# The dilated mixer's tokens ordered by class of 4, and the keys and values of two dilations packed in one block

## The chip, the cores and the metric

The kernel runs on one core of a Trainium2 chip. The metric is the device time of one execution in microseconds (us), the median of three runs. Engines: PE (TensorE matmul; its weight loads are listed apart as PEld), DVE (VectorE), ACT (ScalarE), POOL (GpSimd) and SP (SyncE, which issues most transfers).

## What is computed

A trunk of two layers over 256 tokens of width 2048, 16 heads of 128. Layer 0 is a dilated sliding-window mixer, layer 1 a block-sparse one that with 256 tokens is plain causal attention. Around each: RMS norm, a modulation computed from the vector c, a gate, and at the end a final RMS norm. All inputs are fp32.

```python
DSWA_PATTERNS = ((128, 1), (512, 4), (2048, 16))       # (window, dilation), one per head group

def dilated_mixer(h, w_in, slopes):
    parts = jnp.split(h @ w_in, 3 * N_GROUPS + 1, axis=-1)   # q, k, v of three groups, and z
    for g, (window, dilation) in enumerate(DSWA_PATTERNS):
        o, lse = dilated_window_attention(q_g, k_g, v_g, window, dilation, slopes)
    alpha = jax.nn.softmax(jnp.stack(lses), axis=0)
    o = jnp.einsum('gbsh,gbshd->bshd', alpha, jnp.stack(outs))
    return o * jax.nn.silu(parts[-1])
...
for i in range(DEPTH):
    h = rms_norm(x, norm_w[i]) * (1.0 + scale) + shift
    y = (dilated_mixer(h, a_w_in) if i == 0 else moba_mixer(h, b_w_in)) @ w_out
    x = x + gate * y
return rms_norm(x, final_norm_w)
```

Query t of a group with dilation d attends to t, t-d, t-2d, and so on. Mixing the three groups by their denominators is the same as one softmax over the keys of all three, and the kernel does that.

## The kernel before

**Products.** Nearly all work on PE is the projection of the tokens with fp32 weights. Each operand is split into a high part and a rest (`wh` and `wl`, `hA[.., 0]` and `hA[.., 1]`), and three products in fp32r make one exact enough product. A weight unit of 512 KB is loaded by SP into `raw`, ACT makes `wh` (line 342) and DVE makes `wl` (line 348). The program is a list of steps, each a handful of products on PE; other work (`tasks`, `first_tasks`) is attached to steps by number with `at` and `at_once`, so the order on every engine is that of the code as it is run through at the end (lines 818 to 826).

**Parts and groups of heads.** The 16 heads come in four groups j of four. For every group ten parts are made: v0, v1, v2, z, q0, k0, q1, k1, q2, k2 (the list `PARTS`). A v part has tokens on the partitions (tokens are the stationary operand, `moving`, lines 268 to 270), all others have the head's 128 elements there (`stationary`, 279 to 281, and `stationary_heads`, 292 and 297). The order in `PARTS` sets both the order of work and the buffer that a part lies in. The products sum up in four PSUM banks, `acc`, two for a part at a time (four, one a head, in `stationary_heads`).

**The first 330 us.** The rows of hA appear one after another, since DVE has to sum up the modulation first (`mod_unit`, line 142; `rows_ready`, lines 245 to 257). Until then, parts of the groups 0 and 1 (v0 to k0 of group 1) are worked on in visits: as many rows as are ready for one part, then the next part. At a visit's end `evac_visit` copies the two banks into the part's buffer with ACT (line 560, first visit) or adds them with DVE (line 562, later visits). The first eight visits are one step long each. Later parts are evacuated by `evac` (line 567, ACT).

**An item of the dilated layer.** `item_a` handles one head and one half of the tokens: tt = 0 has the 128 even tokens, tt = 1 the odd ones, so that x is loaded as `x[0].rearrange("(m a) d -> m a d", a=2)`. There are 32 items. A key at a distance that is a multiple of 4 or 16 lies in the same half, so an item has four blocks of 128 keys: both halves for group 0, its own half for group 1 and its own half for group 2. In step s0 PE makes the scores (line 438, into `pss`), DVE adds the distance mask `dm` scaled by the head's slope (401), takes the maximum (403), and ACT the exponent (406). In s1 DVE normalises (414). In s2 PE transposes the four blocks (419) and ACT copies them (421). In s3 PE multiplies them with the values (456, into `po`), DVE gates (458), and `split` writes the two parts of y (189 on ACT, 190 on DVE). The four steps stand apart by the offsets of `item_a`. The items of group 0 stand in the first stretch of group 1, and so on; those of group 3 stand in the output projection.

Of the 128x128 scores of group 1 in such a block only those at a distance of a multiple of 4 count, that is half; for group 2 (multiple of 16) an eighth. The rest is masked.

Of the kernel before, what the change touches and what calls it, by code (L numbers as in the profile page):

```python
# [18 lines left out]
P = 128  # L19
# [13 lines left out]
def distance_masks():  # L33
# [3 lines left out]

    m = np.arange(P)

    def block(tq, tk, rule):  # L40
# [5 lines left out]
    even, odd, low, high = 2 * m, 2 * m + 1, m, m + P  # L46
    cols = [block(even, even, near), block(even, odd, near), block(even, even, every(4)), block(even, even, every(16)),
            block(odd, even, near), block(odd, odd, near)]
# [5 lines left out]
def trunk_kernel(ctx: ExitStack, tc: tile.TileContext, x, c, small_w, mod_t, weights, final_norm_w, dmask, out, laid_out):  # L54
# [23 lines left out]
    x_v = x[0].rearrange("(m a) d -> m a d", a=2)  # L78
# [13 lines left out]
    dm = const.tile([P, 9 * P], F32, name="dm")  # L92
# [93 lines left out]
    def split(dst, src):  # L186

        hi = dst[:, :, 0]
        nc.scalar.activation(hi, src, AF.Copy)
        nc.vector.tensor_tensor(dst[:, :, 1], src, hi.bitcast(F32), op=ALU.subtract)  # L190
# [233 lines left out]
    def item_a(j, hh, tt, base, offsets):  # L424
# [4 lines left out]
        blocks = [(0, slice(0, S)), (1, tok), (2, tok)]  # L429
        order = blocks if tt == 0 else blocks[1:] + blocks[:1]  # L430
        parts = [slice(0, 512)]

        def s0():
            ps = ps_s.tile([P, 512], F32, name="pss", tag="s")
            n = 0
            for g, ks in order:
                w = ks.stop - ks.start
                nc.tensor.matmul(ps[:, n:n + w], heads_of("A", j, f"q{g}")[:, hh, tok],  # L438
                                 heads_of("A", j, f"k{g}")[:, hh, ks], start=True, stop=True)
                n += w  # L440
            st["t"] = tp.tile([P, 512], F32, name="t")
            st["l"] = bias_exp(ps, dm[:, 256 * tt:256 * tt + 512], SLOPES[head], parts, st["t"])
# [4 lines left out]
        def s2():  # L447
            st["pT"] = transpose_p(st["t"], 4)

        def s3():  # L450
            po = ps_o.tile([P, 512], F32, name="po", tag="o")
            vs = []
            for g, ks in order:
                vs += [tokens_of("A", j, f"v{g}", hh)[:, a] for a in ((0, 1) if g == 0 else (tt,))]
# [4 lines left out]
            split(y_of("A", j)[:, hh:hh + 1, :, tt::2], y[:, None, 0:P])  # L459
# [4 lines left out]
    def item_b(j, hh, base, offsets):  # L464
# [5 lines left out]
        def s0():  # L470
# [5 lines left out]
            st["l"] = bias_exp(ps, dm[:, 768:1152], SLOPES[head], parts, st["t"])  # L476
# [22 lines left out]
    PARTS = ["v0", "v1", "v2", "z", "q0", "k0", "q1", "k1", "q2", "k2"]  # L499
# [55 lines left out]

# [309 lines left out]
```

## Time and profile before

| | |
|---|---|
| median of 3 runs | 1576.88 us (1575.72 to 1578.0) |
| the profiled execution | 1577.62 us |
| its span in the trace | 1575.6 us |
| PE busy | 1553.2 us (99%) |
| DVE busy | 1123.7 us (71%) |
| ACT busy | 759.9 us (48%) |
| moved by DMA | 380.77 MB, mean 242 GB/s |

Busy times are unions of the instructions' intervals. A matmul's record is longer than the time after which the next one can start, since matmuls are pipelined; the cost of a matmul is read from the distance between starts. An fp32 matmul (not fp32r) leaves two records on PE and two on PEld, a transpose one on each. In a timeline, equal instructions that follow one another are merged into one row with their number.

### The profile page before, as it was taken

To read this page: it belongs to the slowest core of one execution; us is meant where nothing else is said; L and a number is where in the kernel's file an instruction comes from. 1 tells how busy PE (TensorE), PEld (TensorE's weight loads), DVE (VectorE), ACT (ScalarE), POOL (GpSimd) and SP (SyncE) were. 2 spreads that over 40 slices of the span, in tenths; PEclk is the share of its full clock that TensorE was granted. 3 is DMA by queue.
4 is the path that set the end of the run, shared out by engine and by line. 5 is a ranking of instruction groups with operands and counts; after the bars stand their busy time and mean duration, and the time that the engine had idled before them with its cause. 6 is when DMAs were issued, how large, how long until landed. Compare 5 with 4: busy or idle time off the path is not lost.

```text
span 1575.6 us, 23685 instructions
## 1 busy us (share of the span) xinstructions
PE 1553.2 (99%) x8958; PEld 1363.6 (87%) x8958; DVE 1123.7 (71%) x1998; ACT 759.9 (48%) x1049; POOL 32.2 (2%) x35
## 2 busy tenths in 40 slices
PE   8999999999999999999999999999999999999997
PEld 6898899998988888888888888887888888888886
DVE  7889888978767766677766675766458788565665
ACT  7644444444435544444544444554445555455543
POOL 5000000000000000000000000000000000000000
PEclk9999999999999999999999999999999999999998
DMA  9988998875888567877577876465367897855553
GB/s 349 344 284 311 319 316 277 287 262 191 267 228 323 182 213 250 286 258 259 191 233 259 278 264 209 137 222 168 134 201 233 290 319 253 229 176 199 186 174 107
DMA packets 104758, 380.77 MB, mean 242 GB/s; under 512 B 11714, under 2 KB 11842, under 8 KB 104388
## 3 DMA queue, kind: packets, MB, share of 16 engines
q1 hardware_dynamic: 102528, 372.95, 70.9%
q0 software_dynamic: 1536, 5.26, 0.9%
q8 instruction: 70, 1.15, 0.3%
q10 hardware_dynamic: 580, 1.06, 0.2%
q14 instruction: 44, 0.36, 0.1%
HBM read 377.10 MB, written 2.11 MB: 241 GB/s over the span
## 4 chain that ended last, share of the span: by engine, by line
PE 87%; DVE 3%; ACT 1%; DMA 1%; issue 1%; POOL 0%; POOLq 0%; DVEq 0%; ACTq 0%
PE acc L292 27%; PE acc L297 14%; PE acc L270 10%; PE acc L268 10%; PE acc L269 10%; PE acc L280 4%; PE acc L281 4%; PE acc L279 4%; PE po L456 1%; PE pss L438 1%; PE pst L419 1%; DVE wl L348 1%; DMA raw<-in_weights_dram 1%; PE po L489 1%; PE pss L473 1%
## 5 line engine op out<-in xcount | busy, mean ns | idle before, releaser
L342 ACT ACTIVATE wh<-raw 128x1024 fp32r<-128x1024 f32 (+1 forms) x505 | 527.4, 1056 | 521.8 <-PE acc L292 180.2
L348 DVE TENSOR_TENSOR wl<-raw,wh 128x1024 fp32r<-128x1024 f32 (+1 forms) x505 | 609.7, 1221 | 204.7 <-ACT wh L342 203.6
L292 PE MATMUL acc<-hA,wh 128*128 128x512 f32 x1152 | 288.3, 392 | 1.4 <-DVE actA1q L543 1.4
L292 PEld LDWEIGHTS acc<-hA,wh 128*128 128x128 f32 x1152 | 207.0, 189 | 38.2 <-DVE actA1q L543 1.7
L292 PE MATMUL acc<-hB,wh 128*128 128x512 f32 x768 | 196.4, 395 | 0.0
L279 PE MATMUL acc<-hA,wh 128*128 128x256 f32 x640 | 182.8, 286 | 1.0 <-ACT hA L251 1.0
L280 PE MATMUL acc<-hA,wh 128*128 128x256 f32 x640 | 182.0, 284 | 0.7 <-DVE hA L257 0.6
L281 PE MATMUL acc<-hA,wl 128*128 128x256 f32 x640 | 181.8, 284 | 0.0
L297 PEld LDWEIGHTS acc<-hA,wl 128*128 128x128 f32 x1152 | 157.3, 190 | 11.7
L297 PE MATMUL acc<-hA,wl 128*128 128x256 f32 x1152 | 160.7, 282 | 0.0
L292 PEld LDWEIGHTS acc<-hB,wh 128*128 128x128 f32 x768 | 137.5, 189 | 24.0
L268 PE MATMUL acc<-wh,hA 128*128 128x512 f32 x384 | 155.5, 405 | 1.6 <-DVE hA L253 1.6
L270 PE MATMUL acc<-wh,hA 128*128 128x512 f32 x384 | 151.0, 393 | 0.3 <-DVE hA L257 0.2
L269 PE MATMUL acc<-wl,hA 128*128 128x512 f32 x384 | 150.9, 393 | 0.0
L142 DVE CUSTOM_DVE_ANT_0 raw<-raw,cb 128x512 f32<-128x512 f32 x198 | 131.2, 689 | 9.9 <-DMA raw<-in_mod_t_dram 9.9
L279 PEld LDWEIGHTS acc<-hA,wh 128*128 128x128 f32 x640 | 123.5, 193 | 1.4 <-ACT hA L251 1.2
L280 PEld LDWEIGHTS acc<-hA,wh 128*128 128x128 f32 x640 | 123.4, 193 | 1.3 <-DVE hA L257 1.0
L281 PEld LDWEIGHTS acc<-hA,wl 128*128 128x128 f32 x640 | 123.5, 193 | 0.0
L297 PEld LDWEIGHTS acc<-hB,wl 128*128 128x128 f32 x768 | 105.2, 190 | 8.4 <-DVE wl L348 0.3
L297 PE MATMUL acc<-hB,wl 128*128 128x256 f32 x768 | 108.3, 283 | 0.1
L270 PEld LDWEIGHTS acc<-wh,hA 128*128 128x128 f32 x384 | 72.5, 189 | 16.7 <-DVE hA L257 1.2
L268 PEld LDWEIGHTS acc<-wh,hA 128*128 128x128 f32 x384 | 72.6, 189 | 16.3 <-ACT hf L254 2.4
(228 smaller groups left out, 1779.6 us busy)
## 6 DMA issues: line engine op xcount, KB each, us to landing
raw<-in_weights_dram SPq DMA_DIRECT2D x512, 512.0 KB, 4.5
raw<-in_mod_t_dram SPq DMA_DIRECT2D x132, 512.0 KB, 4.7
gate<-in_mod_t_dram SPq DMA_DIRECT2D x40, 512.0 KB, 5.4
dm<-in_mod_t_dram SPq DMA_DIRECT2D x20, 512.0 KB, 5.1
xin<-in_x_dram SPq DMA_DIRECT2D x2, 1024.0 KB, 6.0
gate<-gate_rows POOLq DMA_DIRECT2D x4, 512.0 KB, 8.4
x<-in_x_dram POOLq DMA_DIRECT2D x4, 512.0 KB, 7.5
fw<-in_final_norm_w_dram POOLq DMA_DIRECT2D x2, 512.0 KB, 5.4
```

The lines of the kernel that those rows point to most:

```text
L142: nc.vector.tensor_tensor_reduce(part, part, cb[q], 1.0, 0.0 if q else mbT[:, m:m + 1], ALU.mult, ALU.add, modq[:, m, q:q + 1])
L268: nc.tensor.matmul(o, hi, wh[:, i], start=f, stop=False, skip_group_check=True)
L269: nc.tensor.matmul(o, hi, wl[:, i], start=False, stop=False, skip_group_check=True)
L270: nc.tensor.matmul(o, lo, wh[:, i], start=False, stop=l, skip_group_check=True)
L279: nc.tensor.matmul(o, wh[:, i, wc], hi, start=first and h % 2 == 0, stop=False, skip_group_check=True)
L280: nc.tensor.matmul(o, wh[:, i, wc], lo, start=False, stop=False, skip_group_check=True)
L281: nc.tensor.matmul(o, wl[:, i, wc], hi, start=False, stop=last, skip_group_check=True)
L292: nc.tensor.matmul(ps_of(h), ws[u][0][:, i, cols(h)], both, start=us[u] == 0 and i == 0, stop=low_first and us[u] == 7 and i == 1, skip_gr ...
L297: nc.tensor.matmul(ps_of(h)[:, 0:S], ws[u][1][:, i, cols(h)], st(2 * us[u] + i)[:, 0, :], start=False, stop=not low_first and us[u] == 7 a ...
L342: nc.scalar.activation(wh[:, c], raw[:, c], AF.Copy)
L348: nc.vector.tensor_tensor(wl[:, c], raw[:, c], wh[:, c].bitcast(F32), op=ALU.subtract)
L419: nc.tensor.transpose(pt[:, b * P:(b + 1) * P], t[:, b * P:(b + 1) * P], ident)
```

## The change

The 256 tokens of the two halves are put in another order: within a half (even or odd tokens), first the 64 tokens with t mod 4 = a, then the 64 with t mod 4 = 2 + a. Two tokens at a distance that is a multiple of 4 or 16 are now always in the same 64. For the groups 1 and 2 therefore only scores of 64 queries with 64 keys are made, and the four 64x64 results of an item are packed into one block of 128x128: for the first 64 queries (class 0) the keys of group 1 and then those of group 2, for the second 64 (class 1) those of group 2 and then those of group 1. An item has three blocks rather than four.

The values of the groups 1 and 2 are packed to match. The buffer of v1 gets the 64 rows of class 0 of both groups, the buffer of v2 those of class 1. `pieces` yields for each PSUM bank of v1 or v2 the two halves of 64 partitions with their destinations, and both `evac_visit` and `evac` go through them, so such a bank is evacuated by two instructions rather than one. In `PARTS`, z moves up to stand behind v0, so v1 and v2 follow each other with z ahead of them. x is loaded by four transfers of 64 partitions instead of two of 128, and y is written back with a stride of four tokens and not two.

```diff
-    even, odd, low, high = 2 * m, 2 * m + 1, m, m + P
+    by_class = [4 * (m % 64) + 2 * (m // 64) + a for a in range(2)]
+    even, odd, low, high = *by_class, m, m + P
...
-    x_v = x[0].rearrange("(m a) d -> m a d", a=2)
+    x_v = x[0].rearrange("(s b a) d -> a b s d", a=2, b=2)
...
-        blocks = [(0, slice(0, S)), (1, tok), (2, tok)]
-        order = blocks if tt == 0 else blocks[1:] + blocks[:1]
-        parts = [slice(0, 512)]
+        parts = [slice(0, 384)]
+        own, pack = (0, 2) if tt == 0 else (1, 0)
+
+        def classes():
+
+            for b in range(2):
+                for g in (1, 2):
+                    n = 64 * ((g - 1) ^ b)
+                    yield b, g, slice(tt * P + 64 * b, tt * P + 64 * b + 64), slice(pack * P + n, pack * P + n + 64)
 
         def s0():
             ps = ps_s.tile([P, 512], F32, name="pss", tag="s")
-            n = 0
-            for g, ks in order:
-                w = ks.stop - ks.start
-                nc.tensor.matmul(ps[:, n:n + w], heads_of("A", j, f"q{g}")[:, hh, tok],
-                                 heads_of("A", j, f"k{g}")[:, hh, ks], start=True, stop=True)
-                n += w
+            nc.tensor.matmul(ps[:, own * P:own * P + S], heads_of("A", j, "q0")[:, hh, tok],
+                             heads_of("A", j, "k0")[:, hh, 0:S], start=True, stop=True)
+            for b, g, ks, to in classes():
+                nc.tensor.matmul(ps[64 * b:64 * b + 64, to], heads_of("A", j, f"q{g}")[:, hh, ks],
+                                 heads_of("A", j, f"k{g}")[:, hh, ks], start=True, stop=True, skip_group_check=True)
...
-            st["pT"] = transpose_p(st["t"], 4)
+            st["pT"] = transpose_p(st["t"], 3)
...
-            for n, vv in enumerate(vs):
-                nc.tensor.matmul(po[:, 0:P], vv, st["pT"][:, n], start=n == 0, stop=n == 3)
+            v = tokens_of("A", j, "v0", hh)
+            for b in range(2):
+                c = slice(64 * b, 64 * b + 64)
+                nc.tensor.matmul(po[:, c], tokens_of("A", j, f"v{1 + b}", hh)[:, tt], st["pT"][:, pack, c], start=b == 0,
+                                 stop=False, skip_group_check=True)
+            for a in range(2):
+                nc.tensor.matmul(po[:, 0:P], v[:, a], st["pT"][:, own + a], start=False, stop=a == 1,
+                                 skip_group_check=True)
...
-    PARTS = ["v0", "v1", "v2", "z", "q0", "k0", "q1", "k1", "q2", "k2"]
+    PARTS = ["v0", "z", "v1", "v2", "q0", "k0", "q1", "k1", "q2", "k2"]
...
+    def pieces(l, j, p, ps, n):
+
+
+        if l == "A" and p in ("v1", "v2"):
+            for b, t in enumerate((act_of(l, j, "v1"), act_of(l, j, "v2"))):
+                r = 64 * (b if p == "v1" else 1 - b)
+                yield t[r:r + 64, n * GC:(n + 1) * GC], ps[64 * b:64 * b + 64]
+        else:
+            yield act_of(l, j, p)[:, n * GC:(n + 1) * GC], ps
```

The order of instructions on PE at the first item's scores (q and k of group 0 of heads; the number behind a name is the buffer's), before:

```order
L270 MATMUL acc<-wh,hA 128x512
L438 MATMUL pss<-actA0k_356,actA0q_332 128x256
L438 MATMUL pss<-actA0k_411,actA0q_387 128x128
L438 MATMUL pss<-actA0k_505,actA0q_461 128x128
L268 MATMUL acc<-wh,hA 128x512
```

and now:

```order
L278 MATMUL acc<-wh,hA 128x512
L449 MATMUL pss<-actA0k_362,actA0q_338 128x256
L452 MATMUL pss<-actA0k_417,actA0q_393 64x64
L452 MATMUL pss<-actA0k_511,actA0q_467 64x64
L452 MATMUL pss<-actA0k_417,actA0q_393 64x64
L452 MATMUL pss<-actA0k_511,actA0q_467 64x64
L276 MATMUL acc<-wh,hA 128x512
```

Two matmuls of 128x128 have become four of 64x64, of which the second pair writes the PSUM partitions from 64 on. On PE at the first item's outputs, with the next item's transposes behind them, before:

```order
L270 MATMUL acc<-wh,hA 128x512
L456 MATMUL po<-pT,actA0v_246 128x128 x2
L456 MATMUL po<-pT,actA0v_260 128x128
L456 MATMUL po<-pT,actA0v_279 128x128
L419 MATMUL pst<-ident,t 128x128 x4
L268 MATMUL acc<-wh,hA 128x512
```

and now:

```order
L289 MATMUL acc<-hA,wl 128x256
L468 MATMUL po<-pT,actA0v_287 128x64
L468 MATMUL po<-pT,actA0v_288 128x64
L471 MATMUL po<-pT,actA0v_248 128x128 x2
L427 MATMUL pst<-ident,t 128x128 x3
L287 MATMUL acc<-hA,wh 128x256
```

The packed values come first and move 64 columns each, and one transpose is gone. On ACT at the first visits (the evacuations of v0, v1, v2 and z of group 0, among the conversions `wh` and the copies of the transposed x), before:

```order
L560 ACTIVATE actA0v_246<-acc 128x512 x2
L560 ACTIVATE actA0v_260<-acc 128x512 x2
L342 ACTIVATE wh<-raw 128x1024
L560 ACTIVATE actA0v_279<-acc 128x512 x2
L238 ACTIVATE xnT_104<-pxt 128x3x128 x2
L560 ACTIVATE actA0z<-acc 128x512 x2
L342 ACTIVATE wh<-raw 128x1024
L560 ACTIVATE actA0q_332<-acc 128x512 x2
```

and now:

```order
L587 ACTIVATE actA0v_248<-acc 128x512 x2
L587 ACTIVATE actA0z<-acc 128x512 x2
L350 ACTIVATE wh<-raw 128x1024
L587 ACTIVATE actA0v_287<-acc 64x512
L587 ACTIVATE actA0v_288<-acc 64x512
L587 ACTIVATE actA0v_287<-acc 64x512
L587 ACTIVATE actA0v_288<-acc 64x512
L246 ACTIVATE xnT_104<-pxt 128x3x128 x2
L587 ACTIVATE actA0v_287<-acc 64x512
L587 ACTIVATE actA0v_288<-acc 64x512
L587 ACTIVATE actA0v_287<-acc 64x512
L587 ACTIVATE actA0v_288<-acc 64x512
```

z now comes ahead of v1 and v2, and each of these two has four evacuations instead of two.

## Rows read from the trace of the kernel before

**Rows 1.** The page: engines' busy time, and the shares of the last chain.

```profile
PE 1553.2 (99%) x8958; PEld 1363.6 (87%) x8958; DVE 1123.7 (71%) x1998; ACT 759.9 (48%) x1049; POOL 32.2 (2%) x35
...
PE 87%; DVE 3%; ACT 1%; DMA 1%; issue 1%; POOL 0%; POOLq 0%; DVEq 0%; ACTq 0%
```

**Rows 2.** Windows: length, then each engine's busy us (instructions), granted clock, DMA, GB/s.

```profile
20.00:30.00 10.00, 10.00 (x69) 9.24 (x68) 10.00 (x17) 9.81 (x19) 10.00 (x5) 0.93 0.94 342
...
80.00:90.00 10.00, 10.00 (x86) 10.00 (x85) 10.00 (x19) 4.57 (x5) 0.00 (x0) 1.00 0.70 248
90.00:100.00 10.00, 8.43 (x55) 8.03 (x55) 8.77 (x22) 3.10 (x4) 0.00 (x0) 0.83 0.97 337
...
300.00:310.00 10.00, 10.00 (x86) 10.00 (x85) 9.85 (x15) 4.55 (x5) 0.00 (x0) 1.00 0.80 266
...
380.00:390.00 10.00, 8.37 (x68) 7.81 (x66) 7.65 (x18) 4.27 (x7) 0.00 (x0) 1.00 0.52 172
...
560.00:740.00 180.00, 180.00 (x1018) 157.74 (x1018) 119.85 (x202) 80.34 (x100) 0.00 (x0) 1.00 0.76 256
```

**Rows 3.** Timeline of PE at an item's scores, then outputs and transposes: start, length.

```profile
335.28 1.04 PE L438 MATMUL pss<-actA0k,actA0q 128*128 128x256 f32 x6
...
336.39 0.39 PE L269 MATMUL acc<-wl,hA 128*128 128x512 f32 x1
...
349.14 0.39 PE L270 MATMUL acc<-wh,hA 128*128 128x512 f32 x1
349.37 1.05 PE L456 MATMUL po<-pT,actA0v 128*128 128x128 f32 x8
350.26 0.60 PE L419 MATMUL pst<-ident,t 128*128 128x128 f32 x4
...
350.93 0.40 PE L269 MATMUL acc<-wl,hA 128*128 128x512 f32 x1
```

**Rows 4.** Timeline where PE restarts, and durations by line (ns, minimum/median/maximum).

```profile
388.34 0.38 PE L456 MATMUL po<-pT,actA0v 128*128 128x128 f32 x1 [0.54 <-ACT pT L421]
388.34 0.19 PEld L456 LDWEIGHTS po<-pT,actA0v 128*128 128x128 f32 x1 [0.75 <-ACT pT L421]
388.45 0.19 PEld L456 LDWEIGHTS po<-pT,actA0v 128*128 128x128 f32 x1
390.16 0.30 PE L419 MATMUL pst<-ident,t 128*128 128x128 f32 x1 [0.66 <-DVE t L414]
390.13 0.20 PEld L419 LDWEIGHTS pst<-ident,t 128*128 128x128 f32 x2 [0.82 <-PE po L456]
...
L456 PE MATMUL po<-pT,actA0v x64: 270/275/377, 349.4 to 395.7; 128*128 128x128 f32 x64
L419 PEld LDWEIGHTS pst<-ident,t x176: 138/141/144, 343.7 to 1501.8; 128*128 128x128 f32 x176
```

**Rows 5.** Groups of instructions by line and shape: busy us, mean ns of one.

```profile
L403 DVE TENSOR_REDUCE m<-t 128x1 f32<-128x512 f32 x32 | 22.0, 686 | 1.1
L401 DVE SCALAR_TENSOR_TENSOR t<-dm,pss 128x512 f32<-128x512 f32 x32 | 21.9, 685 | 18.4 <-PE pss L438 18.3
L562 DVE TENSOR_TENSOR actA0v<-actA0v,acc 128x512 f32<-128x512 f32 x18 | 11.6, 683 | 1.1 <-PE acc L270 1.1
L401 DVE SCALAR_TENSOR_TENSOR t<-dm,pss 128x384 f32<-128x384 f32 x16 | 8.8, 553 | 8.2 <-PE pss L473 8.2
L560 ACT ACTIVATE actA0v<-acc 128x512 f32<-128x512 f32 x6 | 3.3, 593 | 0.2
```

**Rows 6.** Timeline of DVE and ACT at 94 us.

```profile
94.27 0.16 DVE L148 TENSOR_REDUCE modc<-modq 128x2 f32<-128x8 f32 x1
...
94.66 0.60 ACT L251 ACTIVATE hA<-xnT,modc,sc 128x256 fp32r<-128x256 f32 x1 [2.25 <-DVE sc L247]
```

**Rows 7.** Timeline of SP and DVE at the start.

```profile
1.17 0.92 SPq L796 DMA_DIRECT2D xin<-in_x_dram  x2
...
10.21 0.75 DVE L142 CUSTOM_DVE_ANT_0 raw<-raw,cb,smalls 128x512 f32<-128x512 f32 x1 [1.02 <-ACT cb L111]
```

More of the change, by code (lines that the diff above doesn't have):

```diff
@@ L45, in distance_masks @@
     every = lambda n: (lambda d: (d >= 0) & (d % n == 0))
-    even, odd, low, high = 2 * m, 2 * m + 1, m, m + P
-    cols = [block(even, even, near), block(even, odd, near), block(even, even, every(4)), block(even, even, every(16)),
-            block(odd, even, near), block(odd, odd, near)]
+    by_class = [4 * (m % 64) + 2 * (m // 64) + a for a in range(2)]
+    even, odd, low, high = *by_class, m, m + P
+    packed = np.empty((P, P), np.float32)
+    for b in range(2):
+        r = slice(64 * b, 64 * b + 64)
+        t = even[r]
+        for n, rule in enumerate((every(4), every(16))[::1 - 2 * b]):
+            packed[r, 64 * n:64 * n + 64] = block(t, t, rule)
+    cols = [block(even, even, near), block(even, odd, near), packed, block(odd, even, near), block(odd, odd, near)]
     cols += [block(q, k, lambda d: d >= 0) for q, k in ((low, low), (high, low), (high, high))]
@@ L91, in trunk_kernel @@
     gate = [const.tile([P, 1024], F32, name=f"gate{i}") for i in range(2)]
-    dm = const.tile([P, 9 * P], F32, name="dm")
+    dm = const.tile([P, 8 * P], F32, name="dm")
     ones = const.tile([P, P], F32, name="ones")
@@ L184, in rstd_of, with split @@
         return r
-    def split(dst, src):
-        hi = dst[:, :, 0]
+    def split(dst, src, low=None):
+        parts = [dst[:, :, i] if low is None else dst[:, i] for i in range(2)]
+        hi = parts[0]
         nc.scalar.activation(hi, src, AF.Copy)
-        nc.vector.tensor_tensor(dst[:, :, 1], src, hi.bitcast(F32), op=ALU.subtract)
+        nc.vector.tensor_tensor(parts[1], src, hi.bitcast(F32), op=ALU.subtract)
     start_r = []
@@ L475, in s0 @@
             st["t"] = tp.tile([P, 512], F32, name="t")
[L476 removed]
+            st["l"] = bias_exp(ps, dm[:, 640:1024], SLOPES[head], parts, st["t"])
         def s1():
@@ L554, in whole_part @@
         return i
[L556 to L562 removed]
+    def pieces(l, j, p, ps, n):
[5 more added lines that the diff above has]
+            yield act_of(l, j, p)[:, n * GC:(n + 1) * GC], ps
+    def evac_visit(key, j, p, first):
+        for n, bank in enumerate(groups[key]):
+            for dst, ps in pieces("A", j, p, bank, n):
+                if first:
+                    nc.scalar.activation(dst, ps, AF.Copy)
+                else:
+                    nc.vector.tensor_tensor(dst, dst, ps, op=ALU.add)
     def evac(l, j, p):
[L565 to L567 removed]
+        for n, bank in enumerate(groups[l, j, p]):
+            for dst, ps in pieces(l, j, p, bank, n):
+                nc.scalar.activation(dst, ps, AF.Silu if p[0] == "z" else AF.Copy)
     def silu_in_place(l, j, p):
@@ L795, in trunk_kernel @@
     for tt in range(2):
-        nc.sync.dma_start(xin[tt], x_v[:, tt])
+        for b in range(2):
+            nc.sync.dma_start(xin[tt][64 * b:64 * b + 64], x_v[tt, b])
     start_rstd(0)
```

18 lines of the change are left out of this document (4 added, 14 removed).

## The prediction

> **What bounds the kernel now.** I read the busy shares of the engines first, then the table by stretches, then single items of the dilated layer on TensorE. PE is busy 99% of the span, and 87% of the chain that ended last is PE; DVE has 3% of it [rows 1]. By stretches, PE is busy in the whole of 560 to 740 us, with DVE at two thirds and ACT below half [rows 2]: there, a nanosecond of PE is a nanosecond of the end, and nothing that DVE or ACT saves is worth anything. The granted clock is 1.00 (2.4 GHz) in all stretches but the first and the one at 90 us. Two kinds of place are different. From 20 to 30 us ACT is nearly full, and at 80 to 90 us DVE is completely full; PE then stands for part of 90 to 100 us. And at 380 to 390 us PE is idle for 1.6 us, because the first eight items hang on DVE there: at 390 us PE waits for the normalised scores of line 414 [rows 4]. So the change has to be costed as PE time in the items, and as ACT and DVE time in the first 400 us.
>
> **What an item costs PE.** The dilated layer has 32 items. One fp32 matmul is two records on PE. In rows 3 the scores start at 335.28 us and the second product behind them at 336.39 us; with 0.23 us for the product between (349.14 to 349.37), the three score matmuls cost 0.88 us. The four output matmuls are 8 records from 349.37 to 350.26 us: 0.111 us each. The four transposes are one record each, 0.11 us apart. I need to know whether 0.111 us is the time of the moving columns or of loading the weights. Rows 4 tell it, at 388.34 us, where PE had stood idle: the first weight load begins at 388.34, its matmul lasts 0.38 us instead of the usual 275 ns, so it waited some 0.10 us for the weights, and the second load begins 0.11 us after the first. A 128-column weight load therefore takes 0.107 us by itself, as much as 128 moving columns. For a transpose it is less: after the idle time at 390.13 us two loads of 141 ns span 0.20 us, so they stand 0.06 us apart.
>
> **Step 1, one transpose less.** Each item transposes three blocks of 128 instead of four: 32 x 0.109 = -3.5 us of PE. This is the only sure gain.
>
> **Step 2, the outputs.** The two packed output matmuls move 64 columns instead of 128, but their weights (the values) are still 128 columns wide. Their four records go from 0.107 us of streaming to 0.053 us, while loading the next weights still takes 0.107 us. With the load as the floor [rows 4], 8 records remain at 0.11 us: 0. If the load did not hold, it would be -4 x 0.053 x 32 = -6.8 us; I take 0, since the idle start shows the load alone.
>
> **Step 3, the packed scores.** Two matmuls of 128x128 (4 records, 4 x 0.111 = 0.445 us) become four of 64x64 (8 records). Moving 64 columns takes half of 0.107 us; no row shows a 64-column load, so a record lies between 0.054 us (half of everything) and 0.109 us (a load as long as that of 128 columns). The nearest row is the short load of the transposes, 0.06 us apart [rows 4]; with it, 8 x 0.060 = 0.48 us. Per item that is +0.035 us, between -0.01 and +0.43.
>
> **Step 4, two changes of the array's shape.** The 64x64 matmuls write 64 PSUM partitions each, at 0 or at 64, so they use half of the array's columns; every item goes into that shape and out of it again. The trace shows no such change among busy records: the kernel before has only full-width ones once its products run. The lower bound is the change between fp32 records and the products, which costs nothing: from 349.37 to 350.93 us stand 8 output records, 4 transposes and one product, 1.56 us, and 12 x 0.111 + 0.23 is 1.56 [rows 3]. The upper bound is that PE runs empty and starts again at each change: a record lasts 275 ns while the next would start after 0.111 us, so the tail is 0.165 us, and behind it the first weights load openly, 0.107 us for 128 columns and 0.054 us for 64 [rows 4]. That is 2 x 0.165 + 0.107 + 0.054 = 0.49 us an item. I take the middle, 0.25 us: the load cannot be pulled ahead across the change, and a part of the tail is not waited for. The Trainium skill, "TensorEngine Tiling (Array Packing)", Key Properties, says that a change of tiling mode (not merely of the tile) makes TensorE drain; no row of this trace shows one. By it step 4 would cost the upper bound, by rows 3 nothing.
>
> Steps 1 to 4 make -0.109 + 0 + 0.035 + 0.25 = +0.176 us an item on PE.
>
> **Step 5, where the items stand.** 24 items lie in stretches where PE is full: 24 x 0.176 = +4.2 us. The first eight lie between 335 and 397 us, where DVE carries the chain and PE has 1.6 us of idle time [rows 2]; 8 x 0.176 = 1.4 us of PE fits in there. On DVE each item gets shorter: 384 columns instead of 512 save 0.13 us in the scaled bias (685 against 553 ns) and, by an estimate in the same proportion, as much in the maximum (686 ns) [rows 5], together 8 x 0.26 = -2.1 us, and something in the normalisation. But in the same stretch the two value parts of the second group of heads are now added in four pieces each instead of two, +4 x 0.68 = +2.7 us of DVE. So this stretch I put at 0, between -1.6 and +2 us.
>
> **Step 6, the values' evacuations.** No row shows a piece of 64 partitions; it takes between half of one of 128 and the whole. Durations in rows 5 follow the elements per partition, so I take the whole: 0.6 us on ACT and 0.68 us on DVE. The change has 16 more of them on ACT and 20 more on DVE. Eight of those on ACT belong to the third and fourth group of heads; there the next part's products hide them (the nearest bank is wanted again two heads, some 2.8 us, later); were they not hidden, they would cost up to 8 x 0.6 = 4.8 us. The first four are the trouble: the first visits of the two parts are one step each (six products, 6 x 0.23 = 1.4 us), and their evacuations take 2.4 us instead of 1.2 us on an ACT that is 98% busy from 20 to 30 us [rows 2]. PE must wait for the two banks, or for the hidden rows and weights that ACT makes later: up to +2.4 us. On DVE the next additions of these two parts grow by 4 x 0.68 = 2.7 us; they stand shortly ahead of the stretch in which DVE has no gap, at the end of which PE waits for hA (DVE has summed up the modulation's last pieces by 94.27 us, ACT starts hA at 94.66) [rows 6]. The two delays don't add: a late PE meets late rows there. I take +2 us for both. Later, at 300 to 310 us (DVE 98% [rows 2]), four more additions fall into short visits; +1.5 us, between 0 and 4. Together +3.5 us, between 0 and +7.
>
> **Rest.** Loading x in four transfers rather than two adds two issues of 0.46 us each on SP ahead of the first modulation rows; DVE's first sum of them, at 10.21 us, waits for cb [rows 7], so I put it at 0, at most +0.9 us. The gated output written with a stride of four tokens, the shorter exponent and the shorter copy of the transposed block lie on ACT and DVE beside a full PE: 0.
>
> **Sum.** +4.2 + 0 + 3.5 = +7.7 us. The profiled execution took 1577.62 us (span 1575.6), the median of the runs is 1576.88, less than 0.1% apart, so I add to the median: 1584.6 us.
>
> **Rivals.** (a) The shape changes cost nothing. An item then costs PE -0.074 us, 24 of them -1.8 us, and with step 6 the time is 1578.6 us, inside 0.2%. For it: the fp32 to product change is free in rows 3. (b) PE runs empty at each change, 0.49 us: -0.109 + 0.035 + 0.49 = +0.416 an item, 24 of them +10.0, the first eight no longer fit into PE's idle time (8 x 0.416 - 1.6 = +1.7), with step 6 +15.2: 1592.1 us. For it: a load for half the array cannot sit beside the weights of the full one. The Trainium skill's sentence on the drain, named in step 4, is this rival. (c) Faster: the two column halves run beside each other, so that the packed scores cost 4 x 0.054 instead of 0.445 us (-0.23), with no emptying; with the transpose -0.34 us an item, 24 x -0.34 = -8.1, the first stretch -1.6, step 6 at +3.5: 1570.7 us. It decides once a half's load starts under the other half's matmul. Against it: the records of PE follow one another in every row read. The Trainium skill, same page, Key Properties, says that different tiles can load and multiply in parallel; no run here shows it yet. (d) A 64-column load takes as long as one of 128: step 3 +0.43 us; with free changes 24 x 0.32 = +7.7, with step 6 1588 us.
>
> **Chances.** Forecast (half-priced changes) 0.32, (a) 0.24, (b) 0.20, (c) 0.16, (d) 0.08. A difference under 0.2% (3.2 us) cannot be told from none. A part of (a) falls below it with a small step 6, so: faster 0.20, same 0.25, slower 0.55. The range reaches from (c) to (b): 1570 to 1593 us.
>
> **What would show it.** The number of records from the first 64x64 matmul to the next product, and the gap ahead of each of the two changes (step 4: 0.05 to 0.2 us each if right, 0.2 to 0.27 in (b), none in (a)); the spacing of the eight 64-column records (step 3: 0.06 us); output records still 0.11 us apart though they move 64 columns (step 2; 0.06 would refute it); PE's idle time at 20 to 35, 90 to 100 and 295 to 310 us (step 6). Wrong would be most of all the price of the changes: each 0.1 us there is 24 x 2 x 0.1 = 4.8 us.

## The result, and the profile after

The changed kernel takes 1594.09 us (median, 1592.56 to 1598.31) beside 1576.3 us for the kernel before on the same chip: ratio 1.0113, interval 1.01 to 1.0125, so 17.8 us slower. The direction was forecast. The forecast was 1584.6 us, a loss of 7.7, and its range ended at 1593: the loss is more than twice the forecast, and just outside the range.

Busy times, the chain and the loads of x, from the page of after (to be read beside [rows 1] and [rows 7]):

```profile
PE 1560.4 (98%) x9054; PEld 1357.3 (85%) x9054; DVE 1131.6 (71%) x2018; ACT 763.6 (48%) x1065; POOL 31.0 (2%) x35
PE 78%; DVE 4%; issue 2%; ACT 1%; DMA 1%; POOL 0%; POOLq 0%; DVEq 0%; ACTq 0%
xin<-in_x_dram SPq DMA_DIRECT2D x4, 512.0 KB, 8.0
```

The page of before has for the last line:

```profile
xin<-in_x_dram SPq DMA_DIRECT2D x2, 1024.0 KB, 6.0
```

The transfers are half as large, and each takes 8.0 us from its issue to its landing where before it took 6.0. PE's share of the chain falls from 87 to 78%: there are more places at which PE waits for somebody. What PE waits for (line waited for, total, times, longest), in after:

```profile
PE pxt L227 <- ACT xin L223: 4.7, 2, 3.7
PE acc L287 <- ACT hA L259: 4.1, 1, 4.1
PE acc L305 <- DVE wl L356: 3.7, 1, 3.7
```

and of the first two in before:

```profile
PE pxt L219 <- ACT xin L215: 1.0, 1, 1.0
PE acc L279 <- ACT hA L251: 1.0, 1, 1.0
```

Following the same product through both traces, counted from the first, tells where the loss arises. After is behind by 5.0 us at the first product, 7.8 at 36 us (on the clock of the kernel before), 10.1 at 67 to 84, 14.5 at 99 to 111, 16.5 at 232 to 256 and 17.6 at 397 us, where the first eight items are done. Their last output record starts at 395.7 us in before [rows 4] and at 413.3 us in after (minimum, median and maximum length in ns, then the first and the last start):

```profile
L471 PE MATMUL po<-pT,actA0v x32: 275/275/328, 367.3 to 413.3; 128*128 128x128 f32 x32
```

From there to the end nothing is added, but for a single late transfer in this execution, which was the longest of the four: a piece of the modulation's matrix issued at 476.31 us landed 12.98 us later, DVE waited for it, and PE then waited for `wl` (the third of the waits above). That puts 3.5 us on the profiled execution. So **the whole loss lies ahead of 400 us, and the 24 items in which PE is the bound cost next to nothing**.

The first products, after and then before (start, duration, instruction, idle time and releaser):

```profile
8.99 1.23 DVE L209 CUSTOM_DVE_ANT_0 sq<-xin 128x1024 f32<-128x1024 f32 x1 [8.99 <-DMA xin<-in_x_dram]
22.27 0.77 PE L276 MATMUL acc<-wh,hA 128*128 128x512 f32 x1 [2.12 <-DVE hA L261]
```

```profile
6.15 1.23 DVE L201 CUSTOM_DVE_ANT_0 sq<-xin 128x1024 f32<-128x1024 f32 x1 [6.15 <-DMA xin<-in_x_dram]
17.25 0.47 PE L268 MATMUL acc<-wh,hA 128*128 128x512 f32 x1 [1.64 <-DVE hA L253]
```

Stretches of after (busy us of PE, PEld, DVE, ACT and POOL, each with its count, then granted clock, DMA share and GB/s):

```profile
0.00:10.00 10.00, 7.16 (x8) 2.49 (x8) 1.01 (x1) 3.64 (x5) 0.91 (x9) 1.00 0.80 173
30.00:40.00 10.00, 9.15 (x67) 8.21 (x66) 6.96 (x15) 9.84 (x18) 3.81 (x2) 1.00 0.97 349
40.00:50.00 10.00, 9.73 (x72) 8.97 (x71) 6.87 (x15) 9.82 (x18) 0.00 (x0) 1.00 0.49 168
100.00:110.00 10.00, 5.50 (x36) 5.01 (x36) 8.74 (x18) 3.10 (x4) 0.00 (x0) 0.85 0.84 272
```

At 0 to 10 us DMA moves 173 GB/s, where before it moved 302:

```profile
0.00:10.00 10.00, 7.16 (x8) 2.49 (x8) 2.94 (x8) 3.49 (x5) 1.46 (x10) 1.00 0.79 302
```

At 30 to 50 us ACT is full, and in the second half of that the DMA engines are busy for only 0.49 of the time. At 100 to 110 us PE stands for 4.5 us, and the granted clock is 0.85 there, much as in the stretch in which before waited, 90 to 100 us (0.83 [rows 2]). The lower clock is no part of the difference between these two executions: in windows of 10 us up to 420 us it is 0.90, 0.93 and 0.83 in three windows of before and 0.85 and 0.81 in two of after, and what is missing to 1.00 sums to 3.4 us in both. What fills ACT, in after's timeline:

```profile
29.33 2.41 ACT L587 ACTIVATE actA0v<-acc 64x512 f32<-64x512 f32 x4
31.76 0.87 ACT L246 ACTIVATE xnT<-pxt 128x384 f32<-128x384 f32 x2
32.66 2.42 ACT L587 ACTIVATE actA0v<-acc 64x512 f32<-64x512 f32 x4
```

**The item on PE**, after (to be read beside [rows 3]; the last row is of PEld):

```profile
352.27 0.59 PE L449 MATMUL pss<-actA0k,actA0q 128*128 128x256 f32 x2
352.79 0.46 PE L452 MATMUL pss<-actA0k,actA0q 128*64 128x64 f32 x8
353.18 0.50 PE L276 MATMUL acc<-wh,hA 128*128 128x512 f32 x1
353.52 0.40 PE L277 MATMUL acc<-wl,hA 128*128 128x512 f32 x1
...
352.79 0.32 PEld L452 LDWEIGHTS pss<-actA0k,actA0q 128*64 128x64 f32 x8 [0.33 <-issue]
```

From the scores to the second product behind them it is now 1.25 us (before 1.11), less 0.23 for one product: 1.02 against 0.88. The starts of the ten score records one by one, in ns behind the first, with the two products:

```
256 columns:  0, 215
64x64:        523, 536 | 630, 643 | 688, 701 | 746, 760
products:     911, 1252
```

The eight packed records come in **pairs, 13 ns apart**: the matmul for PSUM partitions 0 to 63 and that for 64 to 127 run side by side, and a pair takes 58 ns. That is 0.23 us for all eight. Around them stand two gaps. On the way in, the first packed record starts 308 ns behind the last wide one, which streams for 215, and the second pair comes 107 ns behind the first instead of 58: 0.14 us. On the way out, the second product starts at 1252 ns; a product streams for 0.23 us, so the first one streamed from 1023 on (its record is longer, since it begins with the wait for its weights), while the last pair ended at 746 + 58 + 13 = 817: 0.21 us. PEld shows why: eight loads of 64 columns begin only at 352.79, when the wide matmuls are through, and the idle time ahead of them has no releaser but "issue".

The outputs and transposes of an item, after:

```profile
366.86 0.56 PE L468 MATMUL po<-pT,actA0v 128*128 128x64 f32 x4
367.26 0.66 PE L471 MATMUL po<-pT,actA0v 128*128 128x128 f32 x4
367.76 0.49 PE L427 MATMUL pst<-ident,t 128*128 128x128 f32 x3
```

Eight output records take 0.90 us (366.86 to 367.76; before 0.89 [rows 3]): they are no shorter for moving 64 columns in half of them. Three transposes stand behind them instead of four. One transpose less and 0.14 us more for the scores make +0.03 to 0.04 us an item. The output matmuls of the last group's items agree, in after and in before, 4.99 and 4.95 us from one item to the next:

```profile
1019.55 0.55 PE L468 MATMUL po<-pT,actA3v 128*128 128x64 f32 x4
1024.54 0.55 PE L468 MATMUL po<-pT,actA3v 128*128 128x64 f32 x4
```

```profile
998.04 1.05 PE L456 MATMUL po<-pT,actA3v 128*128 128x128 f32 x8
1002.99 1.05 PE L456 MATMUL po<-pT,actA3v 128*128 128x128 f32 x8
```

### The profile page after: what moved, and what is told of

It is laid out like the page before. It is cut to its first block, busy times and chain, and to the rows that moved or that the text cites. A ratio compares the mean times of both kernels' runs of the same rounds, so it can differ in the third digit from the quotient of the medians.

```text
span 1596.5 us, 23935 instructions
## 1 busy us (share of the span) xinstructions
PE 1560.4 (98%) x9054; PEld 1357.3 (85%) x9054; DVE 1131.6 (71%) x2018; ACT 763.6 (48%) x1065; POOL 31.0 (2%) x35
## 4 chain that ended last, share of the span: by engine, by line
PE 78%; DVE 4%; issue 2%; ACT 1%; DMA 1%; POOL 0%; POOLq 0%; DVEq 0%; ACTq 0%
PE acc L300 27%; PE acc L305 14%; PE acc L276 8%; PE acc L278 8%; PE acc L277 8%; PE acc L287 2%; PE acc L288 2%; PE acc L289 2%; DVE wl L356 1%; PE pst L427 1%; DMA raw<-in_mod_t_dram 1%; PE po L471 1%; PE pss L449 1%; PE po L506 1%; DVE raw L149 1%
## 5 line engine op out<-in xcount | busy, mean ns | idle before, releaser
L300 PE MATMUL acc<-hA,wh 128*128 128x512 f32 x1152 | 292.3, 395 | 0.0
L287 PEld LDWEIGHTS acc<-hA,wh 128*128 128x128 f32 x640 | 124.4, 194 | 10.1 <-ACT hA L259 4.6
```

What stands on the lines that cost most here:

```text
L287: nc.tensor.matmul(o, wh[:, i, wc], hi, start=first and h % 2 == 0, stop=False, skip_group_check=True)
L300: nc.tensor.matmul(ps_of(h), ws[u][0][:, i, cols(h)], both, start=us[u] == 0 and i == 0, stop=low_first and us[u] == 7 and i == 1, skip_gr ...
```

## The experiments

**The change in parts.** Three kernels each hold one part: the loads of x, the values' evacuations, the items. A fourth, shown first, takes one part away from after instead, by reading x from a copy that is laid out in the order of the classes beforehand.

`after_x_two`:

```diff
-        for b in range(2):
-            nc.sync.dma_start(xin[tt][64 * b:64 * b + 64], x_v[tt, b])
+        nc.sync.dma_start(xin[tt], x_classes[tt])
```

> The changed kernel, with x laid out by class beforehand in memory, so that each half of the tokens is again one transfer to 128 partitions. In the changed kernel the first product starts 5.0 us later than before, since the transfers to 64 partitions land late. Theory A (that start is a loss of its own and carried to the end): 5 us less than the changed kernel, about 1589 us, the first product again at 17 us. Theory B (the later waits for rows would have cost it anyway): at most 2 us less, 1592 us or more.

`before_x_four` (the tokens in before's order, in four transfers of 64 partitions):

```diff
-        nc.sync.dma_start(xin[tt], x_v[:, tt])
+        for b in range(2):
+            nc.sync.dma_start(xin[tt][64 * b:64 * b + 64], x_v[64 * b:64 * b + 64, tt])
```

> The kernel before, with its x loaded by four transfers to 64 partitions, nothing else. Theory A: first product at 22 us rather than 17, +5 us, about 1581 us. Theory B: the first product late, but the end at most +2 us, under 1578.5 us. By the prediction on record (at most two issues more, +0.9 us): 1577 us.

`before_v_halves` (each half keeps its place, so only the number of instructions changes):

```diff
+    def pieces(l, j, p, ps, n):
+        dst = act_of(l, j, p)[:, n * GC:(n + 1) * GC]
+        if l == "A" and p in ("v1", "v2"):
+            for b in range(2):
+                yield dst[64 * b:64 * b + 64], ps[64 * b:64 * b + 64]
+        else:
+            yield dst, ps
```

> The kernel before, with the PSUM banks of v1 and v2 evacuated in two halves of 64 partitions, to where they went before, nothing else. Theory A (the first visits' longer evacuations fill ACT, hold back the conversions and so the buffers that SP waits for, and the modulation rows come late): +8 to +12 us, some 1586 us, with PE waiting for hA near 95 us for some 4 us more than before. By the prediction on record: +3.5 us, 1580 us. Theory C (the items cost the most): +0 to +2 us.

`before_items` (after's items with before's x, `PARTS` and evacuations; it leaves out the order by class, so its output is not the mixer's):

```diff
-    PARTS = ["v0", "z", "v1", "v2", "q0", "k0", "q1", "k1", "q2", "k2"]
+    PARTS = ["v0", "v1", "v2", "z", "q0", "k0", "q1", "k1", "q2", "k2"]
...
-            for dst, ps in pieces("A", j, p, bank, n):
```

> The kernel before with the changed items alone: scores of 64x64 in a packed block, three transposes, packed outputs. x, the order of parts and the evacuations are as before, so the packed values are not those of the classes (v1 and v2 are used as they are) and the tokens are not ordered by class. The trace of the changed kernel gives +0.14 us for an item's scores, -0.11 for the transpose, -0.05 for the outputs. Theory A: -1 to 0 us, about 1576 us. Rival C (a drain at each change of shape, as in the prediction's rival b): +10 us, 1586 us. The prediction on record: +4 us, 1580 us.

| kernel | median, us | before beside it | ratio (interval) |
|---|---|---|---|
| after_x_two | 1589.39 | 1576.96 | 1.0077 (1.0064 to 1.009) |
| before_x_four | 1580.65 | 1576.96 | 1.0022 (1.0013 to 1.0032) |
| before_v_halves | 1594.46 | 1576.96 | 1.0111 (1.0096 to 1.0126) |
| before_items | 1576.29 | 1576.96 | 0.9995 (0.9986 to 1.0004) |

The halved evacuations alone cost as much as the whole change: +17.5 us. The four loads of x cost 3.7 us put in and 4.7 us taken out. The items cost nothing that can be measured. The three parts sum to 20.5 us against 17.8 for the whole. One might take it that the late start is absorbed where PE has to wait for rows of hA anyway; but taking that start out of after gives its 4.7 us back, and what is left, `after_x_two`, stands 12.4 us above before, 4.4 less than the halved evacuations and the items add up to (17.5 - 0.7). The traces place this difference in two stretches. Up to the first output record `after_x_two` falls 11.6 us behind before, `before_v_halves` 13.4 and `before_items` 0.5, so the two parts make 2.3 us more than the whole; z has another place in `PARTS` there, which no run changes alone. From that record to the last output of the eighth item `before_v_halves` loses 3.7 us more (362.8 and 412.9 us beside 349.4 and 395.7 [rows 4]) and `before_items` gains 2.0, while after and `after_x_two` lose 0.1:

```profile
L456 PE MATMUL po<-pT,actA0v x64: 270/275/377, 362.8 to 412.9; 128*128 128x128 f32 x64
```

In the changed kernel the items' shorter rows on DVE thus take up what the halved additions cost in that stretch. In `before_v_halves` PE is 2.2 us behind at 36 us, 7.6 at 110, 10.8 at 208 to 300 and 17.1 at 397; from there to the end of the items it loses 0.3 us more, so the halved evacuations of the third and fourth group of heads are hidden. What PE waits for there:

```profile
PE pst L419 <- DVE t L414: 3.4, 3, 2.2
PE acc L279 <- ACT hA L251: 3.2, 1, 3.2
PE acc L268 <- ACT hA L251: 3.0, 2, 2.4
```

The rows of hA come from ACT, but ACT was not late by itself: it needs the modulation that DVE sums up. So which engine's pieces cost it?

**ACT's pieces or DVE's.** `halves_first_only` uses `pieces` at the first visits alone (ACT, 8 more copies there), `halves_adds_only` at the later additions alone (DVE, 20 more); in both, the evacuations of the third and fourth group are whole:

```diff
-            for dst, ps in pieces("A", j, p, bank, n):
+            for dst, ps in (pieces("A", j, p, bank, n) if first else [(whole_buffer, bank)]):
```

```diff
-            for dst, ps in pieces("A", j, p, bank, n):
+            for dst, ps in (pieces("A", j, p, bank, n) if not first else [(whole_buffer, bank)]):
```

(`whole_buffer` stands for `act_of("A", j, p)[:, n * GC:(n + 1) * GC]`.)

> The kernel before with halves of 64 partitions only where ACT copies the first visits of v1 and v2 (eight copies more, up to 60 us); the later additions on DVE and the later evacuations are whole. Evacuating all of them in halves cost 17.5 us. Theory A (ACT in the first 60 us holds back SP and so the modulation rows): most of the 17.5 us, 8 us or more, about 1587 us. Theory B (DVE's additions are the load, since DVE is nearly full up to 400 us): +3 us, 1580 us.

> The kernel before with halves of 64 partitions only in the additions on DVE of the later visits of v1 and v2 (twenty more, 13.7 us of DVE); the first visits and the later evacuations are whole. Theory A: +3 to +5 us, 1581 us. Theory B: +10 to +14 us, as much as DVE's added work, 1589 us.

Measured: 1581.42 us, ratio 1.0028 (1.0018 to 1.0039), and 1592.08 us, ratio 1.01 (1.0087 to 1.0114), beside 1576.0. DVE's additions carry it: by the ratios +15.8 us to +4.4, by the medians +16.1 to +5.4. Of the smaller loss, in the profiled execution 1.8 us stand at 397 us and 1.9 more are a late transfer at 477 us. What an addition of half the partitions costs, from after's groups of instructions by form (busy, mean ns):

```profile
L589 DVE TENSOR_TENSOR actA0v<-actA0v,acc 64x512 f32<-64x512 f32 x24 | 16.4, 685 | 0.4
L589 DVE TENSOR_TENSOR actA0v<-actA0v,acc 128x512 f32<-128x512 f32 x6 | 3.9, 683 | 1.1 <-PE acc L278 1.1
L587 ACT ACTIVATE actA0v<-acc 64x512 f32<-64x512 f32 x8 | 4.7, 592 | 0.1
```

A half takes as long as the whole, so 20 more additions are 20 x 0.685 = 13.7 us of DVE, and they cost 15.8 us of the end. The interval of the ratio is 13.7 to 18.0 us, so this is their own time or somewhat more. By place it is not even. Four additions, 2.7 us, are added at each of five places, and the lag behind before grows by 4.1 us around those at 74 to 84 us, by nothing around those at 148 to 161, by 4.6 at 195 to 211, by 2.7 at 300 to 308 and by 3.7 at 377 to 395. PE's waits are followed by a lower clock in the profiled execution (0.77 at 100 to 110 us, 0.85 at 200 to 210), but that does not set the loss: the four executions had mean granted clocks of 0.992, 0.996, 0.996 and 0.995 and took 1592.12, 1592.18, 1591.26 and 1592.03 us. PE's waits in `halves_adds_only`:

```profile
PE acc L279 <- ACT hA L251: 3.3, 1, 3.3
PE pst L419 <- DVE t L414: 2.7, 2, 2.2
PE acc L268 <- ACT hA L251: 2.4, 1, 2.4
```

**Is DVE then the bound of the first 400 us?** If it were, taking additions away should gain about as much as adding them cost. `no_v_additions` leaves out DVE's later additions of v1 and v2 (these two then hold their first visit alone):

```diff
-            else:
+            elif p not in ("v1", "v2"):
```

> The kernel before without DVE's additions of the later visits of v1 and v2 (20 of 0.683 us, 13.7 us of DVE between 70 and 410 us left out, so v1 and v2 of the first two groups hold their first visit alone). Adding as much work cost 15.8 us. Theory A (DVE has just room enough in the kernel before; PE is the bound, and waits for DVE for some 5 us there): -2 to -4 us, 1573 us. Theory B (DVE is the bound of the first 400 us): -10 us or more, 1566 us.

Measured: 1572.1 us, ratio 0.9972 (0.996 to 0.9984), 4.3 us less (2.5 to 6.3 by the interval). The same 13.7 us of DVE cost 15.8 when added and give back 4.3 when removed. The stretch from 200 to 300 us shows the reason, in before, `halves_adds_only` and `no_v_additions` in this order:

```profile
200.00:300.00 100.00, 100.00 (x755) 96.47 (x754) 85.77 (x161) 41.31 (x43) 0.00 (x0) 1.00 0.88 295
```

```profile
200.00:300.00 100.00, 97.41 (x716) 93.11 (x715) 84.89 (x161) 41.22 (x44) 0.00 (x0) 0.98 0.85 290
```

```profile
200.00:300.00 100.00, 100.00 (x755) 96.47 (x755) 82.78 (x153) 42.08 (x44) 0.00 (x0) 1.00 0.84 295
```

In before PE is full there and DVE at 86%; with the added pieces PE has holes while DVE is no fuller. In before the two engines are nearly balanced: DVE has just enough room to be on time. What is removed then gains only at the two places where PE did wait (2.7 us by 99 us, 2.4 more by 397 us); what is added is, in sum, paid in full.

**Does the place matter?** `after_x_two_v_last` puts v1 and v2 at the end of `PARTS`, where fewer of their visits lie in the early stretch:

```diff
-    PARTS = ["v0", "z", "v1", "v2", "q0", "k0", "q1", "k1", "q2", "k2"]
+    PARTS = ["v0", "z", "q0", "k0", "q1", "k1", "q2", "k2", "v1", "v2"]
```

> The changed kernel with x in two transfers from a copy laid out by class, and with v1 and v2 at the end of the list of parts, so that they are visited three times in the first group of heads and not at all in the second: 4 copies on ACT more than before in the visits (at steps 8 and 10, two steps each) and 8 additions on DVE instead of 20. Both theories of the evacuations: 1576 to 1581 us, some 10 us less than with x alone mended; if the loss were in the items or in the order of values, it would stay near 1589 us.

Measured: 1580.03 us, ratio 1.0027 (1.0016 to 1.0038). It ran on another chip than `after_x_two`; each beside the before of its own chip, it loses 4.0 us against 12.4. With eight additions more on DVE in place of 20, and four copies more on ACT in place of eight, it loses a third as much.

**Two halves of the partitions, or four transfers?** `x_by_columns` keeps four transfers of the same size, but with all 128 partitions and half the columns:

```diff
-        nc.sync.dma_start(xin[tt], x_v[:, tt])
+        for b in range(2):
+            nc.sync.dma_start(xin[tt][:, 1024 * b:1024 * b + 1024], x_v[:, tt, 1024 * b:1024 * b + 1024])
```

> The kernel before, with x loaded by four transfers of 128 partitions x 1024 columns instead of two of 128 x 2048: as many transfers and bytes each as the four of 64 partitions, which cost 4.8 us at the first product and 3.7 at the end. Theory A (it is the 64 partitions): first product at 17 to 18 us, 1576 to 1578 us. Theory B (it is the number of transfers): first product near 22 us, 1580 us.

Measured: 1577.56 us, ratio 1.0003 (0.9994 to 1.0012): no difference. The first 10 us, `x_by_columns` and then `before_x_four`:

```profile
0.00:10.00 10.00, 7.16 (x8) 2.49 (x8) 2.94 (x8) 3.37 (x5) 1.46 (x10) 1.00 0.79 275
```

```profile
0.00:10.00 10.00, 7.16 (x8) 2.48 (x8) 1.17 (x2) 3.63 (x5) 0.91 (x9) 1.00 0.78 172
```

At the same DMA share (0.78 and 0.79) all transfers together move 172 GB/s while x goes to 64 partitions at a time, against 275. The packets of x show it alone: in the first 10 us a packet of 8192 bytes takes 0.31 us in before and 0.63 us in `before_x_four` (medians of 256 and 201 packets). It is the 64 partitions, not the number of transfers.

**What do the packed scores gain and lose?** `items_full_shape` is `before_items` with the packed scores made for all 128 queries: the same 64 moving columns, but no change of the array's shape (and half of each result is overwritten).

```diff
-                nc.tensor.matmul(ps[64 * b:64 * b + 64, to], heads_of("A", j, f"q{g}")[:, hh, ks],
+                nc.tensor.matmul(ps[:, to], heads_of("A", j, f"q{g}")[:, hh, tok],
```

> As before_items (the changed items alone, 1576.3 us), but each of the four packed score matmuls takes all 128 queries as weights and 64 keys as moving columns, so that the array keeps its full shape; the second pair overwrites what the first wrote, so the scores are not the reference's. By the trace of the changed kernel the two changes of shape cost 0.36 us an item and the eight 64-column records 0.23 us, two by two side by side. Theory A (a 128-column weight load is the floor, 0.107 us a record, and no change costs anything): the four matmuls take 8 x 0.11 = 0.87 us, +0.28 us an item over before_items, some +6 us, 1582 us. Rival (records run at 0.054 us as soon as no change stands in the way): -0.16 us an item, -4 us, 1572 us.

Measured: 1585.17 us, ratio 1.0054 (1.0042 to 1.0067), 9.2 us above the before beside it, on another chip than `before_items`, which is 0.7 below its own. PE in it:

```profile
517.39 0.59 PE L449 MATMUL pss<-ext 128*128 128x256 f32 x2
517.82 1.00 PE L452 MATMUL pss<-actA1k,actA1q 128*128 128x64 f32 x8
518.62 0.48 PE L276 MATMUL acc<-wh,hA 128*128 128x512 f32 x1
518.94 0.39 PE L277 MATMUL acc<-wl,hA 128*128 128x512 f32 x1
```

1.55 less 0.23 is 1.32 us, 0.30 more than with 64x64: there is no gap ahead of the packed records (517.82 is 0.43 us behind the first wide one, as two wide ones take), but from the second on each starts 0.11 us behind the last, though it moves 64 columns. So 64x64 is worth its two changes of shape, and the floor of a full weight load is confirmed on the scores as well.

**A version without the cost.** `packed_late` computes all that the change computes, with x from the ordered copy. The visits evacuate whole banks; for the first two groups of heads, three ACT copies of 64x1024 exchange the rows once the last visit of v2 is done:

```diff
-                    n = 64 * ((g - 1) ^ b)
+                    n = 64 * (g - 1)
...
+        nc.scalar.activation(kept[0:64], t2[0:64], AF.Copy)
+        nc.scalar.activation(t2[0:64], t1[64:128], AF.Copy)
+        nc.scalar.activation(t1[64:128], kept[0:64], AF.Copy)
```

`packed_late_pairs` issues the scores of both halves of the tokens together, so that the shape changes twice a head instead of twice an item:

```diff
+            if tt == 0:
+                both = [ps_s.tile([P, 512], F32, name="pss", tag="s"), ps_y.tile([P, 512], F32, name="pss", tag="y")]
+                mine = [pair.pop(0), pair.pop(0)]
+                for n in range(2):
+                    for m, ps in zip(mine, both):
+                        m[n](ps)
```

> The changed kernel with x in two transfers from a copy laid out by class, and the visits of v1 and v2 evacuated whole; when both are complete, three copies of 64x1024 on ACT exchange the rows of one class, for the first two groups of heads (the other two are packed at their evacuation as in the change). All that the change computes, without the 20 additions more. Theory A (the evacuations in halves and the start are the whole loss): as before_items, 1575 to 1577 us. Rival (something else in the change costs, hidden in the sum): 1579 us or more.

> As packed_late, and the scores of both halves of a head's tokens are made in one place on PE: two matmuls of 256 columns, then eight of 64x64, so that the array changes its shape twice a head instead of twice an item. The second scores lie in the bank that was free (ps_y). By the trace a pair of changes costs 0.36 us; 16 pairs less, 12 of them in stretches where PE is full: -4 to -6 us against packed_late, 1570 to 1572 us. Rival (the changes' gaps aren't on the path, or what is gained comes back as DVE's waits): 1575 us or more.

Measured: 1575.6 us, ratio 0.9988 (0.9977 to 0.9999), and 1573.33 us, ratio 0.9975 (0.9964 to 0.9985), beside 1576.37. The second beats both kernels, by 3 us over before, but with x put in order outside the measured time; loading x in four transfers of 64 partitions cost 3.7 to 4.7 us above. Its gain over the first, 2.3 us by the medians, is about half of what was expected of it, and the two intervals overlap. PE in `packed_late_pairs`:

```profile
516.26 1.02 PE L449 MATMUL pss<-ext 128*128 128x256 f32 x4
517.22 0.73 PE L454 MATMUL pss<-actA1k,actA1q 128*64 128x64 f32 x16
517.88 0.50 PE L275 MATMUL acc<-wh,hA 128*128 128x512 f32 x1
518.22 0.40 PE L276 MATMUL acc<-wl,hA 128*128 128x512 f32 x1
```

Two items' scores take 1.96 - 0.23 = 1.73 us instead of 2 x 1.02: 0.31 us a head. Twelve heads whose items stand where PE is full would make 3.7 us. In the profiled executions 3.2 of them are gained between 480 and 1080 us, and 1.2 us go again at 1092 us: PE has waited 1.25 us for `diag`, the products behind that stand 0.43 us apart instead of 0.23, and the granted clock of 1080 to 1100 us is 0.91, in `packed_late` 1.00.

## Why the prediction was right and wrong, step by step

- **Step 1 (one transpose less): right**, by the three transposes in the timeline.
- **Step 2 (outputs stay at 0.11 us): right.** The eight records take as long as before, to 0.01 us. `items_full_shape` shows the same floor on the scores.
- **Step 3 (packed scores, +0.035): wrong in its mechanism.** I let the eight records follow one another, 8 x 0.060 = 0.48 us. They run two by two, 4 x 0.058 = 0.23 us, so the step is -0.21 us. This is the half of rival (c) that I left out of the forecast, and the rows read spoke against it only because none of them held two halves. The Trainium skill, "TensorEngine Tiling (Array Packing)", Key Properties, says that tiles load and multiply in parallel; the pairs 13 ns apart agree.
- **Step 4 (two shape changes, +0.25): right in kind, 0.36 in size** (0.14 in, 0.21 out, and 0.01 by which the two halves of the last pair stand apart), between the middle and the upper bound of 0.49. The Trainium skill, "TensorEngine Tiling (Array Packing)", Key Properties, has the rule that a change of tiling mode drains TensorE. The trace agrees: there is a gap at each change, and `items_full_shape`, which has no change, has none. The bound from the restart in [rows 4] was too high for the two together. Steps 1 to 4 together: -0.109 + 0 - 0.21 + 0.36 = +0.04 us an item instead of +0.176; the distance between two items of the last group, 4.99 against 4.95 us, says the same. The error of step 3 was the larger, and step 4's went the other way.
- **Step 5 (items, +4.2): therefore 24 x 0.035 = +0.8.** `before_items` measures -0.7 us, its interval from -2.2 to +0.6. That the first eight items cost nothing was right, and so was the reason, two terms of DVE against each other: the added pieces cost 3.7 us there alone (`before_v_halves`), the shorter rows gain 2.0 alone (`before_items`), and together, in after, the stretch costs 0.1 us.
- **Step 6 (evacuations, +3.5, at most +7): the step that failed.** Alone it measures +17.5 us. The durations were right (0.685 and 0.592 us for half the partitions), the counts too. Wrong was the way of pricing: I looked for single places where PE would wait for a late bank or row, and let 20 additions vanish wherever PE was full. The additions near 80 us were put at +2 together with ACT's copies, those at 300 us at +1.5; in `halves_adds_only` they cost 4.1 and 2.7 us, and those at 195 to 211 us, which had no term in the sum, 4.6. PE was full because DVE was just on time, as `halves_adds_only` and `no_v_additions` together bear out. 13.7 us more on an engine that is 86 to 89% busy from 60 to 400 us, whose results (rows of hA, weights, the items' normalisation) PE consumes in order, push the later results back; only around 150 us does PE not feel it. ACT's share was nearer to the forecast: +4.4 to +5.4 us, a late transfer in it, against a part of the +2; that the eight later copies are hidden was right.
- **"Rest" (x in four transfers, 0 to +0.9): wrong too**, +3.7 to +4.7. I counted the issue on SP alone and took it that the bytes would arrive as before. `x_by_columns` shows that the number of transfers is indeed free, and that 64 partitions are what costs: 0.63 us a packet in place of 0.31.
- **Rival (b)** gave 1592.1 us, near the result, but by 0.42 us an item that did not occur; the number was right for a reason that was wrong.

What is settled: the size of each part and the engine on which the evacuations act. Not settled is how the loss divides exactly between the late hA rows and the late weights, and why the parts' sum exceeds the whole: the lags show where, but no run changes the place of z alone, and the parts' intervals, some 1.5 us on either side for the two smaller and 2.4 for the largest, are as large as the 2.7 us of difference.

## What to carry to other kernels

Before adding work to an engine "off the path", ask how full it is over the whole stretch and who consumes its results in order: here, at 86 to 89% busy, 13.7 us added came back as 15.8 at the end, while removing the same time gained 4.3. Splitting an instruction into two by partitions doubled its cost on DVE and ACT here (685 against 683 ns and 592 against 593 for half and whole), and a transfer to half the partitions took 0.63 us a packet in place of 0.31; put such a split where it is done once (`packed_late`), not in every accumulating visit. When small matmuls are packed into parts of the array, group them, so that the shape changes seldom: that was worth 0.31 us of PE for each pair of changes spared, and some 2 us at the end.

## What was not expected of the hardware

- Matmuls of 64x64 into the two halves of the array's columns run in pairs, 13 ns apart, 58 ns a pair; going into that shape cost 0.14 us and out of it 0.21 us among fp32 records at the granted clock of 1.00 (2.4 GHz).
- While x went to 64 partitions at a time, all transfers together moved 172 to 173 GB/s in the first 10 us, to 128 partitions 275 to 302 GB/s, at about the same DMA share (0.78 to 0.80). A packet of 8192 bytes took 0.63 us in place of 0.31.
- The gated output takes longer to write with a stride of four tokens, in two runs of 64, than with a stride of two in one run of 128: 429 against 318 ns on ACT, 397 against 295 on DVE. No run tells the stride from the two runs. After by form:

```profile
L197 ACT ACTIVATE yA<-ysb 128x128 fp32r<-128x128 f32 x32 | 13.7, 429 | 26.8 <-DVE ysb L474 26.3
L198 DVE TENSOR_TENSOR yA<-ysb,yA 128x128 fp32r<-128x128 f32 x32 | 12.7, 397 | 16.1 <-ACT yA L197 16.1
```

What it costs at the end isn't measured by itself; `before_items`, which has it, is no slower than before.
